# A two-layer decoder trunk on one core: from a planned order to the order of the program

## The chip, the core and the metric

The kernel runs on one core of a Trainium2 chip. The core has five engines that work side by side, each through its own list of instructions, in the order of that list: TensorE (PE) multiplies matrices and writes to PSUM; VectorE (DVE), ScalarE (ACT) and GpSimd (POOL) work element by element; SyncE (SP) issues the DMA transfers. POOL cannot read PSUM. Semaphores tie the lists together where one instruction needs the result, or the freed buffer, of another. The metric is the device time of one execution in microseconds (us).

## What is computed

Two layers work on x, 2048 tokens of 1024 channels, in float32. Cut to what matters:

```python
def _even_layer(x, ...):                       # layer 0
    q, k, v, g_a, a_lr, u, sv, g_b = _split(x @ w_in, EVEN_SIZES)
    log_a = log_sigmoid(a_lr @ w_a2 + b_a) / 16.0          # forget gate
    o = _gla(q, k, v, log_a)                   # gated linear attention
    o_a = _head_rmsnorm(o, g) * silu(g_a)
    o_b = _spatial_gating(gelu(u), gelu(sv), ...) * silu(g_b)
    return _layer_norm(ALPHA * x + concatenate([o_a, o_b]) @ w_out, ...)

def _odd_layer(x, positions, ...):             # layer 1
    q, k, v, g_c, p, g_d = _split(x @ w_in, ODD_SIZES)
    o = _retention(_rotary(q), _rotary(k), v)  # S <- gamma^128 S + k^T v per chunk
    o_c = _head_groupnorm(o, g) * silu(g_c)
    o_d = _multiscale_pool(p, w_pool, scale) * silu(g_d)
    return _layer_norm(ALPHA * x + concatenate([o_c, o_d]) @ w_out, ...)
```

The weights are 1024 x 3088 and 1024 x 3072 for the way in, and 1024 x 1024 twice for the way out. GLA's state and the retention's state are carried from each chunk of tokens to the next.

## The kernel before

**Blocks, units, passes.** The tokens are worked in four blocks of 512; each block goes through layer 0 and then layer 1. A layer is a row of products of [512 x 1024] by [1024 x 512], called units, run by `unit` (L159). A unit has four chunks of 128 (tokens or output channels), each a sum over eight slices of the contraction, `kt`. To keep float32's accuracy on the faster format, each operand is held as a rounded part and a rest, and each product is three matmuls (`PASSES`, L147): so a unit is 4 x 8 x 3 = 96 matmuls of 512 columns. With `width=2` two chunks share a sweep over the slices; with `width=1` (the second half of each output projection, and layer 1's q, k) each chunk has a sweep of its own. The order of the units in a block: v with the low-rank gate (272 columns), the other half of v (256 columns), q and k of GLA, sv, u and g_b, g_a ("the GLA gate unit"), the rest of g_b and u, the two halves of the output projection with LayerNorm; then layer 1: q and k, v, pooling with its gate, the retention's gate, pooling again, output projection with LayerNorm.

**Weight slices.** One slice, [128 x 512] of a weight, serves 12 matmuls. `wslice` (L93) fetches it into one of 7 raw buffers and `split` (L85) turns it into the two parts: ACT rounds (L87), DVE or POOL by turns subtracts (L91). The parts lie in `wpool`, 12 tiles. `next_weights` (L120) asks for slices up to 20 ahead; a tile comes free when the last matmul on its slice is through, which is in the last sweep of a unit.

**Pauses.** Small steps are put between the matmuls by `later(fn, delay)` (L129) and `between` (L132), which `product` and `unit` call every 24 matmuls. Such steps are: `turn`, the transposes of a row tile after LayerNorm (L556 to L564, 8 transposes on PE, then ACT and DVE make the two parts) and of layer 1's q and k (L589); the low-rank gate (L407) and the decay (L362: Abs, Exp, Ln on ACT; then per half of the heads a subtraction, a scan and an end on DVE, and three exponentials on ACT, L377 to L389); the attention steps `first` and `outputs` (L329, L334); `sgu` (L504); the gates (L183).

**LayerNorm.** `layer_norm_out` (L189) evacuates each chunk of the output projection on DVE: scale and add (L199), statistics (L200, L203), two steps over 1024 columns (L208, L210). Between the two POOL computes the reciprocal root (L178, L181).

**Attention state.** Each step of four updates the state `s0` or `s1`. In GLA `upd` (L455) decays, adds, and decays again; a third copy of the queries, scaled by the decay at mid-chunk, is made on POOL (L435) and used against the state. In layer 1 the queries carry powers of gamma and the keys the inverse powers (L579).

**What sets the order.** Every engine's list is made at build time by a planner: it takes the program's order as priority, estimates how long each instruction takes, and puts each where it can run by that estimate. So the weight splits, asked for at the start of a unit, are placed wherever the planner sees a free tile and a free engine. The constants, and the cosine and sine tables of the rotary step (L283 to L306, some 20 DVE instructions), stand at the start of the program.

Of the kernel before, what the change touches and what calls it, by code (L numbers as in the profile page):

```python
# [9 lines left out]
F32 = mybir.dt.float32  # L10
# [18 lines left out]
PAD = 480  # L29

# [20 lines left out]
def trunk(ctx, tc, x, xT, pos, wv, w, w_a2, pvec, rowp, sgu_rows, w_sT, w_pool, ropec, poolc, out):  # L51
# [6 lines left out]
    wpool = ctx.enter_context(tc.tile_pool(name="wpool", bufs=12))  # L58
# [9 lines left out]
    ps_s = ctx.enter_context(tc.tile_pool(name="ps_s", bufs=2, space=PSUM))  # L68

# [23 lines left out]
    def wslice(*src):  # L93

        raw = rawp.tile([P, 512], F32, tag="raw", name="raw")
        t = wpool.tile([P, 2, 512], F32R, tag="w", name="wt")
        width, c = src[0].shape[1], 0
        for s in src:
            nc.sync.dma_start(raw[:, c:c + width], s)
            c += width  # L100
        split(raw[:, 0:c], t[:, 0, 0:c], t[:, 1, 0:c])
        return [t[:, :, i * width:(i + 1) * width] for i in range(len(src))]

    def xslice(b, kt, units):
        raw = rawp.tile([P, 512], F32, tag="raw", name="xraw")
        nc.sync.dma_start(raw, xT[b, kt])
        split(raw, units[kt // 4][:, kt % 4, 0, :], units[kt // 4][:, kt % 4, 1, :])

    def act_unit():
        return acts.tile([P, 4, 2, TB], F32R, tag="T", name="T")  # L110
# [6 lines left out]
    ready = []  # L117
# [31 lines left out]
    def product(ps, chunks):  # L149

        for kt in range(KT):
            for p_, (lhs, rhs) in zip(ps, chunks):
                for n, (a, b) in enumerate(PASSES):
                    nc.tensor.matmul(p_, lhsT=lhs(kt, a), rhs=rhs(kt, b),  # L154
                                     start=(kt == 0 and n == 0), stop=(kt == KT - 1 and n == 2))
            if len(ps) > 1 and (kt + 1) % (KT // len(ps)) == 0 and kt < KT - 1:
                between()

    def unit(xs, wt, evac, token_major, width=2, cols=512):  # L159

        def chunk(n):
            sl = slice(n * P, (n + 1) * P)
            if token_major:
                return (lambda kt, a: xs[kt // 4][:, kt % 4, a, sl]), (lambda kt, b: wt[kt][:, b, :])
            return (lambda kt, a: wt[kt][:, a, sl]), (lambda kt, b: xs[kt // 4][:, kt % 4, b, :])

        for n in range(0, 4, width):
            ps = [big() for _ in range(width)]
            product([p_[:, 0:cols] for p_ in ps], [chunk(n + i) for i in range(width)])
            for i, p_ in enumerate(ps):  # L170
                evac(n + i, p_[:, 0:cols])
            between()

    def rstd(dst, var, eps, scale=1.0):

        n = dst.shape[1]
        if scale == 1.0:
# [3 lines left out]
        nc.gpsimd.tensor_tensor(dst, dst, neghalf[:, :n], op=ALU.pow)  # L181

    def gate(dst_u, h, psT, gain, sil):  # L183
# [33 lines left out]
    xunits = [act_unit(), act_unit()]  # L217
    for kt in range(KT):
        xslice(0, kt, xunits)
        ready.extend(wslice(*stream.pop(0)))  # L220
# [25 lines left out]
    nc.sync.dma_start(pv, pvec)  # L246
# [3 lines left out]
    wa2raw = w2("wa2raw")[0:48, 0:256]  # L250
# [521 lines left out]
```

## Time and profile before

| | |
|---|---|
| median of 3 runs | 1538.36 us (1537.05 to 1538.57) |
| the profiled execution | 1536.12 us, its span 1533.7 us |
| PE busy | 1490.2 us, 97% |
| DVE, ACT, POOL busy | 832.4, 568.1, 637.3 us (54%, 37%, 42%) |
| DMA | 162.19 MB, mean 106 GB/s |
| matmuls of L154 | 3456 and 2688, 731.0 and 625.7 us busy |
| weight rounding on ACT (L87, into wt) | 496 instructions, mean 616 ns |
| weight subtraction on POOL, on DVE (L91, into wt) | 252 of mean 1381 ns, 244 of mean 896 ns |

The profile is that of one execution. Its span runs from the first to the last instruction. A busy PE is not PE at its peak, since matmuls are pipelined and their ends are modelled; what PE waits for is read from the idle time ahead of its instructions. A group's row gives the line in the kernel, engine, operation, what it writes and reads, the count, then busy time in us and mean ns of one, then idle time of the engine ahead of it and what ended it. In a timeline a row gives start, length in us, engine, line, operation.

### The profile page before, as it was taken

To read this page: it belongs to the slowest core of one execution; us is meant where nothing else is said; L and a number is where in the kernel's file an instruction comes from. 1 tells how busy PE (TensorE), PEld (TensorE's weight loads), DVE (VectorE), ACT (ScalarE), POOL (GpSimd) and SP (SyncE) were. 2 spreads that over 40 slices of the span, in tenths; PEclk is the share of its full clock that TensorE was granted. 3 is DMA by queue.
4 is the path that set the end of the run, shared out by engine and by line. 5 is a ranking of instruction groups with operands and counts; after the bars stand their busy time and mean duration, and the time that the engine had idled before them with its cause. 6 is when DMAs were issued, how large, how long until landed. Compare 5 with 4: busy or idle time off the path is not lost.

```text
span 1533.7 us, 21008 instructions
## 1 busy us (share of the span) xinstructions
PE 1490.2 (97%) x7728; PEld 1245.4 (81%) x7728; DVE 832.4 (54%) x1491; ACT 568.1 (37%) x949; POOL 637.3 (42%) x568
## 2 busy tenths in 40 slices
PE   7999999999999999999999999999999999989997
PEld 6888877888888887788888888778888888877886
DVE  6554384645745348464574525746466542573635
ACT  4634322333443332324263332323436334232430
POOL 5245433445524443335443443434543444242542
PEclk9999999999999999999999999999999999999999
DMA  7325322234523431323352242131444334223231
GB/s 227 101 83 165 91 75 83 69 104 133 179 69 98 150 111 55 98 68 115 121 179 83 83 160 87 55 110 56 128 136 150 107 100 144 62 69 97 79 94 55
DMA packets 87047, 162.19 MB, mean 106 GB/s; under 512 B 10096, under 2 KB 18336, under 8 KB 86944
## 3 DMA queue, kind: packets, MB, share of 16 engines
q1 hardware_dynamic: 86944, 160.85, 33.9%
q8 instruction: 60, 0.98, 0.3%
q14 instruction: 43, 0.35, 0.1%
HBM read 152.43 MB, written 8.39 MB: 105 GB/s over the span
## 4 chain that ended last, share of the span: by engine, by line
PE 87%; DVE 6%; issue 4%; POOL 2%; ACT 1%; DMA 0%; SPq 0%; POOLq 0%; DVEq 0%; ACTq 0%
PE big L154 77%; PE att L312 4%; DVE wt L91 2%; PE trp L348 1%; PE trp L508 1%; PE trp L560 1%; PE trp L643 1%; DVE ra L584 1%; DVE rows L210 1%; DVE ra L586 0%; DVE ang L299 0%; PE trp L535 0%; PE trp L679 0%; DVE ra L579 0%; DVE alr L403 0%
## 5 line engine op out<-in xcount | busy, mean ns | idle before, releaser
L154 PE MATMUL big<-wt,T 128*128 128x512 f32 (+2 forms) x3456 | 731.0, 371 | 6.2 <-ACT wt L87 4.5
L154 PEld LDWEIGHTS big<-wt,T 128*128 128x128 f32 x3456 | 601.1, 190 | 114.2 <-ACT wt L87 4.5
L154 PE MATMUL big<-T,wt 128*128 128x512 f32 x2688 | 625.7, 391 | 0.0
L154 PEld LDWEIGHTS big<-T,wt 128*128 128x128 f32 x2688 | 500.6, 188 | 106.3 <-issue 2.7
L91 POOL TENSOR_TENSOR wt<-raw,wt 128x512 fp32r<-128x512 f32 (+1 forms) x252 | 345.7, 1381 | 350.5 <-ACT wt L87 350.2
L87 ACT ACTIVATE wt<-raw 128x512 fp32r<-128x512 f32 (+1 forms) x496 | 301.9, 616 | 322.8 <-PE big L154 288.3
L91 DVE TENSOR_TENSOR wt<-raw,wt 128x512 fp32r<-128x512 f32 (+1 forms) x244 | 217.1, 896 | 249.7 <-ACT wt L87 248.6
L91 POOL TENSOR_TENSOR T<-y,T 128x512 fp32r<-128x512 f32 x48 | 61.0, 1289 | 75.9 <-ACT T L87 75.9
L199 DVE SCALAR_TENSOR_TENSOR rows<-rows,big 128x512 f32<-128x512 f32 x64 | 43.6, 683 | 79.9 <-PE big L154 79.9
L178 POOL TENSOR_SCALAR lnrs<-lnmv 128x1 f32<-128x1 f32 x32 | 26.6, 832 | 119.2 <-DVE lnmv L203 119.1
L327 DVE COPY_PREDICATED pm<-mask,att 128x256 f32<-128x256 int32 x64 | 26.0, 440 | 65.4 <-PE att L312 65.4
L562 ACT ACTIVATE T<-trp 128x512 fp32r<-128x512 f32 x32 | 17.5, 596 | 102.0 <-PE trp L560 102.0
L210 DVE SCALAR_TENSOR_TENSOR rows<-rows,lnrs,ln 128x1024 f32<-128x1024 f32 (+1 forms) x36 | 47.1, 1318 | 13.5 <-POOL lnrs L181 11.9
L186 DVE SCALAR_TENSOR_TENSOR y<-trp,pv,sg 128x512 f32<-128x512 f32 x48 | 34.8, 745 | 34.6 <-PE trp L679 17.6
L181 POOL TENSOR_TENSOR rs<-rs,neghalf 128x4 f32<-128x4 f32 x48 | 49.3, 1028 | 4.0
L178 POOL TENSOR_SCALAR rs<-mv 128x4 f32<-128x4 f32 x32 | 7.4, 231 | 100.8 <-DVE mv L488 52.6
L208 DVE SCALAR_TENSOR_TENSOR rows<-rows,lnmv,ln 128x1024 f32<-128x1024 f32 (+1 forms) x36 | 45.2, 1266 | 0.7
L91 POOL TENSOR_TENSOR T<-pd,T 128x512 fp32r<-128x512 f32 x16 | 25.7, 1606 | 42.5 <-ACT T L87 42.5
L200 DVE BATCH_NORM_STATS2 lnst<-rows 128x6 f32<-128x512 f32 x64 | 42.9, 687 | 0.9
L87 ACT ACTIVATE T<-y 128x512 fp32r<-128x512 f32 x48 | 30.4, 632 | 31.2 <-DVE y L186 30.9
L651 ACT ACTIVATE pb<-big 128x512 f32<-128x512 f32 x16 | 9.6, 599 | 85.4 <-PE big L154 78.7
L520 ACT ACTIVATE act<-big 128x512 f32<-128x512 f32 x32 | 19.1, 597 | 52.3 <-PE big L154 51.5
(185 smaller groups left out, 1085.0 us busy)
## 6 DMA issues: line engine op xcount, KB each, us to landing
raw<-in_w SPq DMA_DIRECT2D x448, 256.0 KB, 2.8
xraw<-in_xT SPq DMA_DIRECT2D x32, 256.0 KB, 3.1
rows<-in_x SPq DMA_DIRECT2D x8, 1024.0 KB, 6.0
ln<-in_rowp SPq DMA_DIRECT2D x16, 512.0 KB, 5.6
out<-rows SPq DMA_DIRECT2D x12, 512.0 KB, 2.6
raw<-in_wv SPq DMA_DIRECT2D x32, 136.0 KB, 3.2
raw<-in_wv SPq DMA_DIRECT2D x32, 128.0 KB, 2.6
out<-rows SPq DMA_DIRECT2D x8, 256.0 KB, 2.0
```

The costliest lines, as they stand in the source:

```text
L87: nc.scalar.activation(hi, src, AF.Copy)
L91: eng.tensor_tensor(lo, src, hi.bitcast(F32), op=ALU.subtract)
L154: nc.tensor.matmul(p_, lhsT=lhs(kt, a), rhs=rhs(kt, b), start=(kt == 0 and n == 0), stop=(kt == KT - 1 and n == 2))
L178: nc.gpsimd.tensor_scalar(dst, var, eps, None, op0=ALU.add)
L181: nc.gpsimd.tensor_tensor(dst, dst, neghalf[:, :n], op=ALU.pow)
L186: nc.vector.scalar_tensor_tensor(y, psT, gain, sil, op0=ALU.mult, op1=ALU.mult)
L199: nc.vector.scalar_tensor_tensor(rh, rh, ALPHA, ps, op0=ALU.mult, op1=ALU.add)
L200: nc.vector.bn_stats(sts[t][:, half, :], rh)
L208: nc.vector.scalar_tensor_tensor(row[:, cs], row[:, cs], mv[:, 0:1], gt[:, cs], op0=ALU.subtract, op1=ALU.mult)
L210: nc.vector.scalar_tensor_tensor(row[:, cs], row[:, cs], rs, bt[:, cs], op0=ALU.mult, op1=ALU.add)
L312: nc.tensor.matmul(dst, lhsT=lhsT, rhs=rhs, start=start, stop=stop, skip_group_check=True)
L327: nc.vector.copy_predicated(pm[t % 2][:, r::2, :], mask_b, ps[r][:, 2:4, :])
```

## The change

Each engine now issues in the order in which the program emits its instructions (`tc.manual_schedule()`), and the program is rewritten for that order.

- **Weights.** `fetch` issues one slice's DMA, `cut` splits the oldest one landed and fetches another. `pace`, called after each slice's matmuls, adds a twelfth of a credit per matmul of 512 columns (less for narrower ones), up to 3, and cuts a slice per credit while one of the 12 tiles has room. A unit that finds no slice ready cuts one on the spot. In the second half of each output projection, all subtractions go to POOL (`sub=nc.gpsimd`).
- **Pauses.** The turns after LayerNorm and of layer 1's q, k have delay 3, not 2. The splits of the gates and the SGU are put off by one pause. The decay is in two steps, `decay` up to Ln and `decay2`, which has the subtractions and scans of both halves first and then the exponentials.
- **State.** GLA's state is kept decayed to the middle of the next chunk, so the third copy of the queries and POOL's product go; `upd` is one addition and one multiplication by a joined factor `f`. In layer 1 the queries no longer carry powers of gamma; the group norm takes them out, and its epsilon is scaled instead (`ret_eps`). The q half of the evacuation is a copy on ACT, the k half a multiplication on DVE. In `outputs`, the scaling of the result comes after the mask for the next step.
- **Start.** The first block's x and weight slices are issued first, then the small constants with five weight slices among them; the constants' arithmetic comes in pauses of the second v unit, and the cosine and sine in pauses after GLA's q, k, three instructions at a time.
- **Next x.** The next block's x is fetched two slices ahead and split in four steps of two.

The diff, cut to its core:

```diff
+SLOTS = 12
+    ctx.enter_context(tc.manual_schedule())
...
-    AHEAD = KT + 12
-    def next_weights():
-        while len(ready) < AHEAD and stream:
-            ready.extend(wslice(*stream.pop(0)))
-        return [ready.pop(0) for _ in range(KT)]
...
+    landed, ready = [], []
+    room, credit = [SLOTS], [0.0]
+    cutter = [None]
...
+    def cut():
+        raw, n, width = landed.pop(0)
+        assert room[0] > 0
+        room[0] -= 1
+        t = wpool.tile([P, 2, 512], F32R, tag="w", name="wt")
+        c = n * width
+        split(raw[:, 0:c], t[:, 0, 0:c], t[:, 1, 0:c], cutter[0])
+        ready.extend((t[:, :, i * width:(i + 1) * width], i == n - 1) for i in range(n))
+        fetch()
+    def pace(matmuls):
+        credit[0] = min(credit[0] + matmuls / 12.0, 3.0)
+        while credit[0] >= 1.0 and room[0] > 0 and landed:
+            cut()
+            credit[0] -= 1.0
...
+    def unit(xs, evac, token_major, width=2, cols=512, sub=None):
+        cutter[0] = sub
+        wt = []
+        for n in range(0, 4, width):
+            ps = [big()[:, 0:cols] for _ in range(width)]
+            for kt in range(KT):
+                if len(wt) == kt:
+                    while not ready:
+                        cut()
+                    wt.append(ready.pop(0))
...
+                if n + width == 4 and last:
+                    room[0] += 1
+                pace(3 * width * cols / 512.0)
+                if width > 1 and (kt + 1) % (KT // width) == 0 and kt < KT - 1:
+                    between()
             for i, p_ in enumerate(ps):
-                evac(n + i, p_[:, 0:cols])
+                evac(n + i, p_)
             between()
...
     def gate(dst_u, h, psT, gain, sil):
...
-        split(y, dst_u[:, h, 0, :], dst_u[:, h, 1, :], nc.gpsimd)
+        later(lambda: split(y, dst_u[:, h, 0, :], dst_u[:, h, 1, :], nc.gpsimd))
...
-        unit(xs, next_weights(), lambda t, ps: evac(0, t, ps), True)
-        unit(xs, next_weights(), lambda t, ps: evac(1, t, ps), True, width=1)
+        unit(xs, lambda t, ps: evac(0, t, ps), True)
+        unit(xs, lambda t, ps: evac(1, t, ps), True, width=1, sub=nc.gpsimd)
@@ outputs(t)
-            norm(t, [p_[:, 0:2, :] for p_ in ps])
-            upd(t, u[:, 0:2, :])
+            scale = norm(t, [p_[:, 0:2, :] for p_ in ps])
+            nc.vector.tensor_tensor(state, state, u[:, 0:2, :], op=ALU.add)
+            upd(t)
             if not last:
                 masked(t + 1, ps)
+            scale()
@@ gla_exps (the second part of gla_decay)
+            out.append((tb, ta, e2, ends))
+        for tb, ta, _, ends in out:
             nc.scalar.activation(tb, ta, AF.Exp, scale=1.0 / 16.0)
             nc.scalar.activation(ta, ta, AF.Exp, scale=-1.0 / 16.0)
             nc.scalar.activation(ends, ends, AF.Exp, scale=1.0 / 16.0)
@@ layer0
+        if b == 0:
+            constants()
+            later(constants2, 3)
+            later(constants3, 4)
         later(low_rank, 1)
         later(decay, 2)
-        unit(xs, next_weights(), lambda t, ps: nc.scalar.activation(vt[:, t, 256:512], ps, AF.Copy), True, cols=256)
+        later(decay2, 3)
+        unit(xs, lambda t, ps: nc.scalar.activation(vt[:, t, 256:512], ps, AF.Copy), True, cols=256)
...
-            nc.gpsimd.tensor_tensor(G[:, 3, :].rearrange("p (t c) -> p t c", c=P),
-                                    G[:, 0, :].rearrange("p (t c) -> p t c", c=P),
-                                    ends[:, :, 0:1].broadcast_to([P, NT, P]), op=ALU.mult)
...
-        def upd(t, u):
-            for s in range(2):
-                ends = decays[s][2]
-                nc.vector.scalar_tensor_tensor(s0[:, s, :], s0[:, s, :], ends[:, t, 0:1], u[:, s, :],
-                                               op0=ALU.mult, op1=ALU.add)
-                nc.vector.tensor_scalar(s0[:, s, :], s0[:, s, :], ends[:, t, 1:2], None, op0=ALU.mult)
+        def upd(t):
+            nc.vector.tensor_tensor(s0, s0, f[:, :, t:t + 1].broadcast_to([P, 2, P]), op=ALU.mult)
@@ after, and evac_qk of layer1
-            later(turn, 2)
+            later(turn, 3)
@@ evac_qk of layer1
-            nc.vector.tensor_tensor(a.rearrange("p (h c) -> p h c", c=64), ps.rearrange("p (h c) -> p h c", c=64),
-                                    gam.unsqueeze(2).broadcast_to([P, 8, 64]), op=ALU.mult)
+            nc.scalar.activation(a[:, 0:256], ps[:, 0:256], AF.Copy)
+            nc.vector.tensor_tensor(a[:, 256:512].rearrange("p (h c) -> p h c", c=64),
+                                    ps[:, 256:512].rearrange("p (h c) -> p h c", c=64),
+                                    gam[:, 4:8].unsqueeze(2).broadcast_to([P, 4, 64]), op=ALU.mult)
```

More of the change, by code (lines that the diff above doesn't have):

```diff
@@ L91, in split @@
         eng.tensor_tensor(lo, src, hi.bitcast(F32), op=ALU.subtract)
[L93 to L110, printed above, removed]
     stream = []
@@ L147, in trunk @@
     PASSES = ((0, 0), (0, 1), (1, 0))
[L149 to L165, printed above, removed]
-        for n in range(0, 4, width):
-            ps = [big() for _ in range(width)]
-            product([p_[:, 0:cols] for p_ in ps], [chunk(n + i) for i in range(width)])
+    def unit(xs, evac, token_major, width=2, cols=512, sub=None):
+        cutter[0] = sub
+        wt = []
+        for n in range(0, 4, width):
+            ps = [big()[:, 0:cols] for _ in range(width)]
[4 more added lines that the diff above has]
+                    wt.append(ready.pop(0))
+                t, last = wt[kt]
+                for i, p_ in enumerate(ps):
+                    sl = slice((n + i) * P, (n + i + 1) * P)
+                    xt = xs[kt // 4][:, kt % 4]
+                    for q, (a, b) in enumerate(PASSES):
+                        lhsT, rhs = (xt[:, a, sl], t[:, b, :]) if token_major else (t[:, a, sl], xt[:, b, :])
+                        nc.tensor.matmul(p_, lhsT=lhsT, rhs=rhs, start=(kt == 0 and q == 0),
+                                         stop=(kt == KT - 1 and q == 2))
+                if n + width == 4 and last:
[3 more added lines that the diff above has]
+                    between()
             for i, p_ in enumerate(ps):
-                evac(n + i, p_[:, 0:cols])
+                evac(n + i, p_)
             between()
@@ L272, in trunk @@
     cst = const.tile([P, 4, P], F32, name="cst")
-    sb = w2("sgub")
-    nc.sync.dma_start(sb, sgu_rows[0:1, :].broadcast_to([P, TB]))
-    sbs = w2("sgubs")
-    nc.sync.dma_start(sbs, sgu_rows[1:2, :].broadcast_to([P, TB]))
-    ps = tr()
-    for g in range(4):
-        nc.tensor.matmul(ps[:, g, :], lhsT=sb[:, g * P:(g + 1) * P], rhs=wsT[:, g, :], start=True, stop=True)
-    nc.vector.tensor_tensor(flat(cst), flat(ps), sbs, op=ALU.add)
     cos = const.tile([P, SEQ // P, 32], F32, name="cos")
@@ new lines, in trunk @@
+    wraw, sb, sbs = w2("wraw"), w2("sgub"), w2("sgubs")
+    xunits = [act_unit(), act_unit()]
+    for kt in range(KT):
+        raw = xfetch(0, kt)
+        fetch()
+        xcut(raw, kt, xunits)
+        raw, _, width = landed.pop(0)
+        t = wpool.tile([P, 2, 512], F32R, tag="w", name="wt")
+        split(raw[:, 0:width], t[:, 0, 0:width], t[:, 1, 0:width])
+        room[0] -= 1
+        ready.append((t[:, :, 0:width], True))
+    nc.sync.dma_start(pv, pvec)
+    for i in range(3):
+        nc.sync.dma_start(wa2raw[16 * i:16 * i + 16, :], w_a2)
@@ new lines, in constants2, with constants3 @@
+    def constants2():
+        split(wraw, wp[:, 0, :], wp[:, 1, :], nc.vector)
+        for g in range(4):
+            nc.gpsimd.affine_select(out=wsT[:, g, :], in_=wsT[:, g, :], compare_op=ALU.is_ge, fill=0.0,
+                                    base=0, pattern=[[1, P]], channel_multiplier=-1)
+        nc.vector.scalar_tensor_tensor(ret_eps, gam[:, 4:8], 64.0 * LN_EPS, gam[:, 4:8], op0=ALU.mult, op1=ALU.mult)
+    def constants3():
+        ps = tr()
+        for g in range(4):
+            nc.tensor.matmul(ps[:, g, :], lhsT=sb[:, g * P:(g + 1) * P], rhs=wsT[:, g, :], start=True, stop=True)
+        nc.vector.tensor_tensor(flat(cst), flat(ps), sbs, op=ALU.add)
@@ L341, in outputs @@
                     b0 = 64 * r
-                    mm(ps[r][:, s, :], qk(s, b0, t)[2], state[b0:b0 + 64, s, :], stop=last and s == 1)
+                    mm(ps[r][:, s, :], qk(s, b0, t)[1], state[b0:b0 + 64, s, :], stop=last and s == 1)
             if not last:
@@ L396, in layer0 @@
         alrT = w2("alrT")[0:48, :].bitcast(F32R)
-        als, decays, heads = [], [], {}
+        als, logs, decays, heads = [], [], [], {}
+        f = small.tile([P, 2, NT], F32, tag="f", name="f", bufs=2)
         def evac_v0(t, ps):
```

186 lines of the change are left out of this document (112 added, 74 removed).

## The prediction

> **What bounds the kernel now.** I read the page first, then the waits of TensorE (PE), then the timeline at the places where PE waits and where the new order puts something else in front of it.
>
> ```profile
> span 1533.7 us, 21008 instructions
> ...
> PE 87%; DVE 6%; issue 4%; POOL 2%; ACT 1%; DMA 0%; SPq 0%; POOLq 0%; DVEq 0%; ACTq 0%
> ```
>
> The profiled execution took 1536.1 us, 2.4 above its span and 2.2 below the median of the runs (1538.4). The chain that ended last is PE for 87%. No matmul is added or removed, so only PE's waits can change the time.
>
> ```profile
> PE trp L560 <- issue: 11.4, 4, 2.9
> PE trp L410 <- DVE alr L403: 6.8, 7, 1.3
> PE trp L592 <- DVE ra L586: 5.5, 6, 1.0
> PE big L154 <- ACT wt L87: 4.5, 1, 4.5
> PE trp L592 <- ACT wt L87: 2.0, 2, 1.0
> PE trp L560 <- DVE rows L210: 1.6, 2, 0.8
> PE trp L279 <- POOL wsT L266: 1.6, 1, 1.6
> ```
>
> These are PE's waits: total us, times, longest. The 4.5 is the start, which stays. The other six rows make 28.9 us: the transposes after layer 0's LayerNorm (L560), those of layer 1's queries and keys (L592), the low-rank gate (L410), the SGU constant (L279).
>
> ```profile
> 209.25 5.92 PE L154 MATMUL big<-wt,T 128*128 128x512 f32 x25
> 218.03 1.06 PE L560 MATMUL trp<-ident,rows 128*128 128x128 f32 x8 [2.86 <-issue]
> 218.85 7.33 PE L154 MATMUL big<-wt,T 128*128 128x512 f32 x24
> ```
>
> Columns: start, length, work. After the wait of 2.86, 24 matmuls take 7.33 where 25 took 5.92: 1.6 us of slower clock, which happens behind two of these four waits, 3 us. And the last matmul before a wait is drawn longer than its turn takes, which hides some 0.2 to 0.3 of each of about 25 waits, an estimate of 6. If every wait after the start went, the kernel would lose about 38 us.
>
> **The change part by part.**
>
> *What goes.* The turns (transposes) come a chunk of 24 matmuls, 5.5 us, later; the cosine and sine chain leaves the start; the bursts of weight splitting after a unit end. I count all 38 as removed and add back what I find late in the new order. In the first block PE still waits for its PSUM tiles after the first product, since four evacuations now follow the weight slices on ACT: +2 (0 to 3).
>
> *What paces the weights now.* I followed the credit through the text: a slice is split per 12 matmuls of 512 columns, per 22 or so of the narrower v units. After the two v units only two slices of the next unit (layer 0's q and k) have been issued in blocks 1 and 2, the second of them behind the exponentials; three in block 3 and four in block 0, the last of each behind them too.
>
> ```profile
> 403.04 3.74 ACT L87 ACTIVATE wt<-raw 128x512 fp32r<-128x512 f32 x7
> ...
> 413.39 0.74 ACT L419 ACTIVATE v<-big 128x256 f32<-128x256 f32 x2 [1.92 <-PE big L154]
> 414.17 0.69 ACT L368 ACTIVATE ta<-trp,pv 128x512 f32<-128x512 f32 x1
> 414.87 1.28 ACT L372 ACT_TABLE_LOAD   x1
> 416.17 0.63 ACT L372 ACTIVATE ta<-ta 128x512 f32<-128x512 f32 x1
> ```
>
> ```profile
> 414.30 6.02 PE L154 MATMUL big<-wt,T 128*128 128x256 f32 x48
> 420.16 16.52 PE L154 MATMUL big<-T,wt 128*128 128x512 f32 x72
> ```
>
> ```profile
> 425.86 0.69 DVE L377 TENSOR_TENSOR tb<-tb,ta 128x512 f32<-128x512 f32 x1 [1.00 <-ACT ta L374]
> 426.58 1.22 DVE L378 TENSOR_TENSOR_SCAN ta<-smask,tb 128x512 f32<-128x512 bf16 x1
> 427.84 0.17 DVE L382 COPY ends<-ta 128x8 f32<-128x8 f32 x1
> 428.05 0.43 DVE L384 TENSOR_TENSOR ta<-ta,ends 128x256 f32<-128x256 f32 x1
> ```
>
> Before, seven slices were split in one go at 403, long ahead (first row). Now count from 413.39, the evacuation between the halves of the second v unit. ACT issues, in order: two copies 0.74, two Abs 1.4, a table load 1.28, two Exp 1.26, a load 1.28, two Ln 1.26 (the Exp row's 0.63 each). That is 7.2. Only then comes the rounding of the q unit's first slice, 0.5 to 0.6 (3.74 for seven): 7.8; its subtraction stands on POOL in blocks 1 and 2 and takes 1.38 (the group row below): 9.2. PE is done with the second v unit at 420.16, which is 6.8, and uses the subtracted half two matmuls (0.23 each, 16.52 for 72) later, at 7.2. **First wait: 2.0.**
>
> The second slice stands behind the decay exponentials. DVE can start at the first Ln, 6.6, and needs 2.6 for each of two heads' pairs (four rows above, start to end): 9.2 and 11.8. ACT's last two Exp and a short one end at 13.3, the slice's rounding at 13.9, its subtraction on DVE (0.7) at 14.6. PE, released at 9.2 and busy 0.9, wants that half at 10.5. **Second wait: 4.1**, and 1 to 2 more where POOL's subtraction and DVE's scan get in each other's way (below). I take 6.5 per block for 1 and 2. In block 3 the first two slices are in time and the third has the same place, with its subtraction on POOL: 6.7. In block 0 it is the fourth slice, with constants to split besides: 5. Together **+25 (20 to 29)**. Evacuations queued behind the exponentials free PSUM tiles that PE needs only a pass later. Four waits of 4 us and over would bring the slow clock of 1.6 in most cases: +4 (0 to 10).
>
> ```profile
> 196.85 0.69 DVE L199 SCALAR_TENSOR_TENSOR rows<-rows,big 128x512 f32<-128x512 f32 x1 [2.84 <-PE big L154]
> 197.57 0.69 DVE L200 BATCH_NORM_STATS2 lnst<-rows 128x6 f32<-128x512 f32 x1
> 198.30 0.21 DVE L203 BATCH_NORM_AGGREGATE lnmv<-lnst 128x2 f32<-128x12 f32 x1
> 198.54 1.28 DVE L208 SCALAR_TENSOR_TENSOR rows<-rows,lnmv,ln 128x1024 f32<-128x1024 f32 x1
> 200.62 1.28 DVE L210 SCALAR_TENSOR_TENSOR rows<-rows,lnrs,ln 128x1024 f32<-128x1024 f32 x1 [0.79 <-POOL lnrs L181]
> ```
>
> ```profile
> 213.82 5.24 POOL L91 TENSOR_TENSOR wt<-raw,wt 128x512 fp32r<-128x512 f32 x3
> ```
>
> ```profile
> 215.65 2.28 DVE L210 SCALAR_TENSOR_TENSOR rows<-rows,lnrs,ln 128x1024 f32<-128x1024 f32 x1
> ```
>
> *LayerNorm and layer 1's q, k.* A row tile's LayerNorm takes DVE 5.05 us (196.85 to 201.90) of a pass of 5.5. While POOL subtracts without pause (1.75 each instead of 1.3 to 1.4), the last step takes 2.28 instead of 1.28. The new order puts eight subtractions of the LayerNorm's second unit on POOL, two per pass, right behind the reciprocal root that releases this step. So I count 6.05 a pass: 0.6 of lag per pass, and with the turn's two PSUM subtractions the third turn finds its PSUM tiles taken for about 1 us. Then one slice of layer 1's q, k unit is subtracted on DVE behind all that: 1 to 2.5. **+11 over four blocks** (5 to 22), against 20.5 in the L560 and L592 rows.
>
> *The v unit of the next block.* Its seventh slice is issued behind the last row tile's root on POOL, its eighth behind the last step on DVE; the root ends some 5 us after the pass (0.1 to 3.9 in these rows, plus lag), the subtraction 1.4 later, and PE wants it at 4.5 to 4.8 (36 matmuls of 6.02/48): 1 to 2.7 in three blocks, **+4** (2 to 8).
>
> ```profile
> L91 POOL TENSOR_TENSOR wt<-raw,wt 128x512 fp32r<-128x512 f32 x232 | 329.4, 1430 | 337.2 <-ACT wt L87 336.9
> ...
> L181 POOL TENSOR_TENSOR rs<-rs,neghalf 128x4 f32<-128x4 f32 x48 | 49.3, 1028 | 4.0
> ...
> L469 DVE TENSOR_REDUCE ss<-sq 128x4 f32<-128x512 f32 x16 | 10.9, 684 | 23.3 <-ACT sq L467 23.3
> ...
> L467 ACT ACTIVATE sq<-att 128x256 f32<-128x256 f32 x32 | 10.5, 381 | 38.9 <-PE att L312 38.9
> ```
>
> ```profile
> 125.60 1.54 PE att L312 x16
> ```
>
> *The GLA gate unit.* (Group rows: busy, mean ns; the mean of all slice forms is 1.38.) At its first pause stand the last attention step, then two deferred SGU splits, then the pending weight slices. From the pause: attention 1.54, two squares 0.76, the sum 0.68, the root 1.03 with a short scaling ahead, all waiting for one another: 4.2 on POOL; two SGU subtractions and the seventh slice's, 1.3 to 1.4 each: 8.2. PE wants it 12 matmuls after the attention's 2.1, plus 0.45: 5.3. A wait of 2.9 in blocks 1 and 2, 1.5 in block 0, none in block 3: **+7** (5 to 9). Two smaller places of the same kind (the output projection's fifth slice behind the last SGU split, the gate unit before it): +3 (0 to 3).
>
> *At nothing.* The state's new form saves POOL's product and a DVE pass per step, and moves half of an evacuation to ACT; these lie beside matmuls. If that cover failed, each costs under 1 us per step. Layer 1's other units start with six slices issued, so nothing queued matters there. The cosine and sine steps go three per pause beside the sv unit and the next ones, where DVE has time and nothing waits for them before layer 1. On SP five slices stay in hand; the constants' loads now queue behind the first slices, and stores of the output ahead of later ones for less than a pass.
>
> Sum: -38 + 2 + 25 + 4 + 11 + 4 + 7 + 3 = +18 on the profiled 1536.1, so 1554, and 1556 beside the median.
>
> **A rule that would price it otherwise.** The rows of POOL at 5.24 for three and DVE at 2.28 show both still moving while they overlap, each slowed. The Trainium skill (SBUF — State Buffer, "Who interferes with whom") says that a VectorE instruction with two SBUF inputs and a GpSimd instruction that reads SBUF take the shared port pair in turn, and that the second one is blocked until the first is through. By that rule the last step would wait for a whole subtraction.
>
> **Rivals.**
>
> - *Slower, moderate (the forecast)*: slices reach PE late behind ACT's exponentials. For it: the order of ACT's queue and the durations. Against: nothing in the trace of before shows the order itself.
> - *Faster*: the waits of 38 go, and the order costs less than I count because POOL, DVE and ACT seldom collide (ACT is busy 37%): 20 at the q unit, 5 at the LayerNorm, 2 in the start and v units, 3 at the gate, no slow clock: 1538 - 38 + 30 = 1530. If the slices of the q unit were in time after all, it would be 1510. Deciding point: whether a slice's rounding must wait for the Ln of its block.
> - *Much slower*: POOL and DVE exclude each other in the LayerNorm units. Per pass two steps of 1.28, a root of 0.8 and two subtractions of 1.3 are 6.0 against 5.45, and each blocked step adds 1.3: about 0.6 per pass more than counted, 32 passes, 18 us: 1574. It decides once DVE's row tile exceeds 6.1 us. The skill's rule above would lead here.
> - *It doesn't do what it says*: the written order nearly equals the planner's, or the parts cancel: 1538.
>
> **How the numbers follow.** Forecast 0.49, much slower 0.20, faster 0.25, no change 0.06. About 0.2% (3 us) is what a measurement of this kernel can tell. So slower 0.69, same 0.06, faster 0.25. The forecast alone runs from 1540 to 1572; the range takes in most of the faster case and of the slower: 1518 to 1584.
>
> **What would show it.** Right: PE's waits name ACT's or DVE's weight slices at the start of layer 0's q, k unit, 5 to 8 us per block, with ACT's exponentials just before; L560, L592 and L410 nearly gone. Wrong: no wait of PE over 1 us there, and PE's share above 98%. The LayerNorm step is right if L210 takes 1.8 to 2.3 us in the second unit; the gate step if PE waits for a POOL subtraction some 12 us after it begins.

## The result, and the profile after

The kernel after takes 1588.9 us (median of 4 runs, 1586.3 to 1590.6) where the kernel before takes 1538.2 beside it: a ratio of 1.0329, interval 1.0312 to 1.0347. It is slower, as forecast, but by 51 us where 18 were forecast, and it lies above the range. The profiled execution took 1590.6 us. From its page, the span, the busy time of the engines and the chain that ended last:

```profile
span 1588.9 us, 20834 instructions
...
PE 1515.9 (95%) x7728; PEld 1259.0 (79%) x7728; DVE 841.1 (53%) x1452; ACT 529.6 (33%) x956; POOL 702.0 (44%) x592
...
PE 70%; DVE 9%; POOL 8%; issue 6%; DMA 3%; ACT 2%; SPq 1%; POOLq 0%; ACTq 0%; DVEq 0%
```

PE does the same 7728 matmuls, but is busy 25.7 us longer than before (1490.2), and idle for 73.0 us of its span where it was for 43.5. The waits of PE, total, times, longest:

```profile
PE big L186 <- ACT wt L91: 23.5, 9, 5.6
PE big L186 <- POOL wt L95: 20.7, 17, 3.3
PE big L186 <- DVE wt L95: 10.6, 10, 2.1
PE trp L631 <- DVE T L634: 5.9, 4, 1.5
PE big L186 <- ACT v L464: 3.5, 1, 3.5
```

The waits of before at L560, L592 and L410 are gone, but for the 5.9 at L631, the turn. In their place stands one kind: a weight slice that is not yet rounded (L91) or subtracted (L95). Where the time went, by the kind of unit: from the start of a unit's first matmul to that of the next unit's (for the last one, to the end of the span), summed over the four blocks, in us. The last column is an experiment told below (e14); units that moved by less than 0.5 are left out.

| unit | before | after | e14 |
|---|---|---|---|
| both v units, layer 0 | 116.5 | 114.5 | 112.4 |
| q, k, layer 0 | 89.6 | 118.9 | 91.4 |
| u and g_b, first half | 116.2 | 117.6 | 116.2 |
| GLA gate unit | 103.6 | 117.6 | 103.6 |
| output projection, first half | 87.4 | 99.7 | 87.4 |
| output projection, second half, with LayerNorm | 94.3 | 101.3 | 97.2 |
| q, k, layer 1 | 121.9 | 112.4 | 103.9 |
| v, layer 1 | 108.3 | 105.9 | 106.0 |
| layer 1's output projection, second half | 95.1 | 99.9 | 95.5 |

*Layer 0's q, k unit in block 1.* From the timeline: start, length, engine, line, work, and in brackets the idle time just before with what ended it.

```profile
424.75 1.28 ACT L425 ACT_TABLE_LOAD   x1
427.21 1.28 ACT L427 ACT_TABLE_LOAD   x1
428.50 1.15 ACT L427 ACTIVATE ta<-ta 128x512 f32<-128x512 f32 x2
429.56 0.61 ACT L91 ACTIVATE wt<-raw 128x512 fp32r<-128x512 f32 x1
430.23 0.73 PE L186 MATMUL big<-T,wt 128*128 128x512 f32 x2 [0.64 <-ACT wt L91]
430.25 1.93 POOL L95 TENSOR_TENSOR wt<-raw,wt 128x512 fp32r<-128x512 f32 x1 [11.28 <-ACT wt L91]
432.23 1.20 PE L186 MATMUL big<-T,wt 128*128 128x512 f32 x4 [1.27 <-POOL wt L95]
435.89 0.63 ACT L446 ACTIVATE ta<-ta 128x512 f32<-128x512 f32 x1
436.52 0.61 ACT L91 ACTIVATE wt<-raw 128x512 fp32r<-128x512 f32 x1
437.19 10.17 PE L186 MATMUL big<-T,wt 128*128 128x512 f32 x34 [3.76 <-ACT wt L91]
```

The rounding at 429.56 stands behind two table loads and the Ln at 428.50; PE waits 0.64 for it and 1.27 for its subtraction. The next rounding, at 436.52, stands behind the last exponentials (L446 at 435.89), and PE waits 3.76. POOL had been idle for 11.28: it had no subtraction to do, because ACT had not come to the rounding.

*The clock.* Stretches of that unit: length, PE busy and its matmuls, the granted clock, DMA share, GB/s.

```profile
437.00:444.00 7.00, 6.81 (x20) 0.65 0.51 159
444.00:451.00 7.00, 7.00 (x32) 1.00 0.42 140
```

PE is busy in both, and does 20 matmuls in the first and 32 in the second. Over the whole span, after and then before:

```profile
core 0: 1588.9 us, clock 0.981
```

```profile
core 0: 1533.7 us, clock 0.996
```

An estimate from these two means: a clock lower by 0.019 over 1588.9 is 30.2 us, by 0.004 over 1533.7 it is 6.1. The difference, 24, is nearly all of the 25.7 us by which PE is busy longer.

*The gate unit in block 1.*

```profile
523.28 0.66 ACT L533 ACTIVATE sq<-att 128x256 f32<-128x256 f32 x2 [7.13 <-PE att L363]
523.97 0.69 DVE L535 TENSOR_REDUCE ss<-sq 128x4 f32<-128x512 f32 x1 [4.10 <-ACT sq L533]
524.74 0.19 POOL L205 TENSOR_SCALAR rs<-ss 128x4 f32<-128x4 f32 x1 [6.03 <-DVE ss L535]
525.02 1.29 POOL L206 TENSOR_TENSOR rs<-rs,neghalf 128x4 f32<-128x4 f32 x1
526.28 2.95 POOL L95 TENSOR_TENSOR T<-ys,T 128x512 fp32r<-128x512 f32 x2
529.20 1.26 POOL L95 TENSOR_TENSOR wt<-raw,wt 128x512 fp32r<-128x512 f32 x1
530.51 4.15 PE L186 MATMUL big<-T,wt 128*128 128x512 f32 x10 [3.27 <-POOL wt L95]
```

POOL idles until 524.74 for the sum, then does the root, two SGU subtractions, and last the slice that PE waits for. The ten matmuls after the wait of 3.27 take 4.15, at about half rate.

*The first half of the output projection.*

```profile
568.51 1.28 ACT L591 ACT_TABLE_LOAD   x1 [7.51 <-PE big L186]
573.59 0.63 ACT L91 ACTIVATE T<-ys 128x512 fp32r<-128x512 f32 x1 [2.70 <-DVE ys L584]
576.17 0.63 ACT L91 ACTIVATE T<-ys 128x512 fp32r<-128x512 f32 x1 [1.95 <-DVE ys L584]
576.71 3.74 ACT L91 ACTIVATE wt<-raw 128x512 fp32r<-128x512 f32 x7
577.37 0.49 PE L186 MATMUL big<-wt,T 128*128 128x512 f32 x1 [1.03 <-ACT wt L91]
579.89 10.49 PE L186 MATMUL big<-wt,T 128*128 128x512 f32 x45 [2.02 <-POOL wt L95]
```

ACT waits 2.70 and 1.95 for the products of the last two SGU parts, whose splits stand ahead of seven weight slices in its list; then it does all seven in one go.

*The second half, with the LayerNorm.*

```profile
601.75 0.69 DVE L224 SCALAR_TENSOR_TENSOR rows<-rows,big 128x512 f32<-128x512 f32 x1 [3.38 <-PE big L186]
605.45 1.29 POOL L95 TENSOR_TENSOR wt<-raw,wt 128x512 fp32r<-128x512 f32 x1
605.52 2.31 DVE L235 SCALAR_TENSOR_TENSOR rows<-rows,lnrs,ln 128x1024 f32<-128x1024 f32 x1 [0.79 <-POOL lnrs L206]
606.71 2.28 POOL L95 TENSOR_TENSOR wt<-raw,wt 128x512 fp32r<-128x512 f32 x1
...
613.23 5.73 PE L186 MATMUL big<-wt,T 128*128 128x512 f32 x24
620.42 1.25 PE L631 MATMUL trp<-ident,rows 128*128 128x128 f32 x8 [1.46 <-DVE T L634]
628.77 0.73 PE L186 MATMUL big<-wt,T 128*128 128x512 f32 x2 [1.92 <-DVE wt L95]
630.67 6.81 PE L186 MATMUL big<-wt,T 128*128 128x512 f32 x24
```

DVE's row tile takes 6.08 us (601.75 to 607.83), its last step (L235) 2.31 beside POOL's two subtractions. The third turn waits 1.46, and one slice is late by 1.92.

### The profile page after: what moved, and what is told of

The parts are those of the page before. It is cut to its first block, busy times and chain, and to the rows that moved or that the text cites. A ratio compares the mean times of both kernels' runs of the same rounds, so it can differ in the third digit from the quotient of the medians.

```text
span 1588.9 us, 20834 instructions
## 1 busy us (share of the span) xinstructions
PE 1515.9 (95%) x7728; PEld 1259.0 (79%) x7728; DVE 841.1 (53%) x1452; ACT 529.6 (33%) x956; POOL 702.0 (44%) x592
## 4 chain that ended last, share of the span: by engine, by line
PE 70%; DVE 9%; POOL 8%; issue 6%; DMA 3%; ACT 2%; SPq 1%; POOLq 0%; ACTq 0%; DVEq 0%
PE big L186 61%; PE att L363 4%; DVE rows L235 3%; DMA xraw<-in_xT 3%; POOL wt L95 2%; POOL lnrs L203 2%; POOL T L95 2%; DVE lnst L225 1%; DVE rows L224 1%; POOL lnrs L206 1%; PE trp L399 1%; DVE wt L95 1%; DVE T L634 1%; PE trp L631 1%; DVE ys L584 1%
## 5 line engine op out<-in xcount | busy, mean ns | idle before, releaser
L186 PE MATMUL big<-T,wt 128*128 128x512 f32 x2688 | 642.4, 397 | 29.2 <-ACT wt L91 17.0
L186 PEld LDWEIGHTS big<-T,wt 128*128 128x128 f32 x2688 | 508.5, 191 | 144.0 <-ACT wt L91 19.1
L95 POOL TENSOR_TENSOR wt<-raw,wt 128x512 fp32r<-128x512 f32 (+1 forms) x284 | 401.4, 1424 | 369.8 <-ACT wt L91 363.1
L95 DVE TENSOR_TENSOR wt<-raw,wt 128x512 fp32r<-128x512 f32 x212 | 228.8, 1086 | 181.5 <-ACT wt L91 181.3
L91 ACT ACTIVATE wt<-raw 128x512 fp32r<-128x512 f32 (+1 forms) x496 | 279.5, 610 | 115.3 <-PE big L186 69.7
L224 DVE SCALAR_TENSOR_TENSOR rows<-rows,big 128x512 f32<-128x512 f32 x64 | 43.5, 679 | 89.7 <-PE big L186 89.7
L203 POOL TENSOR_SCALAR lnrs<-lnmv 128x1 f32<-128x1 f32 x32 | 39.9, 1248 | 91.0 <-DVE lnmv L228 91.0
L95 POOL TENSOR_TENSOR T<-y,T 128x512 fp32r<-128x512 f32 x48 | 73.7, 1556 | 8.4 <-ACT T L91 8.4
L235 DVE SCALAR_TENSOR_TENSOR rows<-rows,lnrs,ln 128x1024 f32<-128x1024 f32 (+1 forms) x36 | 64.3, 1785 | 24.9 <-POOL lnrs L206 24.7
L95 POOL TENSOR_TENSOR T<-pd,T 128x512 fp32r<-128x512 f32 x16 | 20.7, 1292 | 64.1 <-ACT T L91 64.1
L533 ACT ACTIVATE sq<-att 128x256 f32<-128x256 f32 x32 | 10.5, 381 | 98.2 <-PE att L363 98.2
L689 DVE BATCH_NORM_STATS2 st<-att 128x6 f32<-128x128 f32 x64 | 14.2, 284 | 54.5 <-PE att L363 54.5
L580 POOL TENSOR_TENSOR act<-act 128x512 f32<-128x512 f32 x16 | 20.4, 1296 | 38.4 <-ACT act L591 38.4
```

The source lines that it names most:

```text
L91: nc.scalar.activation(hi, src, AF.Copy)
L95: eng.tensor_tensor(lo, src, hi.bitcast(F32), op=ALU.subtract)
L186: nc.tensor.matmul(p_, lhsT=lhsT, rhs=rhs, start=(kt == 0 and q == 0), stop=(kt == KT - 1 and q == 2))
L224: nc.vector.scalar_tensor_tensor(rh, rh, ALPHA, ps, op0=ALU.mult, op1=ALU.add)
L235: nc.vector.scalar_tensor_tensor(row[:, cs], row[:, cs], rs, bt[:, cs], op0=ALU.mult, op1=ALU.add)
L580: nc.gpsimd.tensor_tensor(gu, gu, sg, op=ALU.mult)
```

## The experiments

Three theories. **A**: the slices are emitted too late, so that they stand behind other work in the lists of ACT, POOL and DVE. **B**: work that went to POOL collides with DVE. **C**: the rate alone starves PE, whatever ACT has to do. All ratios are to the kernel before, run beside it on the same chip. Of a kernel without a ratio there is a single run, so a few us of it show nothing.

**e1: a whole credit per column tile, however narrow.**

```diff
-                pace(3 * width * cols / 512.0)
+                pace(3 * width)
```

> Theory A (slices are issued too late, behind other work in ACT's and POOL's queues): counting every matmul of the two narrow v units as a full one puts 12 slices instead of 2 to 4 ahead of GLA's q, k, and 10 instead of 4 or 5 ahead of each later unit of layer 0. The q, k units fall from 118.9 us (four blocks) to about 90, the GLA gate units from 117.6 to about 104, the first halves of layer 0's output projection from 99.7 to about 88; in all about 1588.9 - 52 = 1537. Theory B (the work moved to POOL and its collisions with DVE cost the time): the number of subtractions is the same, so the waits stay and the time is above 1575.

1524.3 us, ratio 0.9912 (0.9895 to 0.9929): one expression takes away 65 us, more than the 52 expected. The q, k unit is at 90.1, the gate unit at 103.6, the first half of the projection at 87.4. These three make 55 of the 65. B, the collision of POOL's subtractions with the LayerNorm's row tile, cannot give that: the LayerNorm's second unit itself got only 4.3 shorter, and L235 still takes 2.3 in half of layer 0's row tiles. Block 0's first v unit gets 9 us longer, because its evacuations on ACT now stand behind slices that have not landed.

**e3: the gate's and the SGU's splits at once, not a pause later.**

```diff
-        later(lambda: split(y, dst_u[:, h, 0, :], dst_u[:, h, 1, :], nc.gpsimd))
+        split(y, dst_u[:, h, 0, :], dst_u[:, h, 1, :], nc.gpsimd)
...
-            later(lambda: split(y, cb[:, g, 0, :], cb[:, g, 1, :], nc.gpsimd))
+            split(y, cb[:, g, 0, :], cb[:, g, 1, :], nc.gpsimd)
```

> Splits of the gates and the SGU are issued at once, not a pause later. Theory A: in the GLA gate unit two POOL subtractions (2.95 us) leave the place between the attention step's root and the seventh weight slice, so these units fall from 117.6 to 105 to 108 us and the whole to about 1578; the q, k units stay at 119. Theory B: the same POOL work, so within 3 us of 1589.

1578.1 us. The gate unit goes from 117.6 to 106.6, so the two deferred splits were most of what stood ahead of its slice; the q, k unit stays at 119.1, and the first half of the projection gets longer (102.6).

**e4: the planner back, with the rewritten text.** The line `ctx.enter_context(tc.manual_schedule())` is left out.

> The new text, but ordered by the planner (the one line that asks for the order of the program is left out). Theory A: the planner moves rounding and subtraction of slices ahead of the waiting exponentials; the q, k units come back to about 90, and with the later turns the whole is 1515 to 1540. Theory B (the text's pacing, state and POOL moves are at fault, not the order): above 1570.

1520.3 us, ratio 0.9886 (0.9872 to 0.9901). The text is no loss under the planner; the text taken as the order is.

**e5: no Exp and Ln in the decay, and so no table loads there.** The three Exp and the Ln of the decay become Abs.

> The decay's Exp and Ln are replaced by Abs, which needs no table load; the decay comes out as a constant, so the output is not the reference's. Theory A: ACT's chain ahead of the first late slice is two loads (2.56 us) shorter and that ahead of the second about as much; the first wait of the q, k unit goes and the second falls from 3.9 to about 1.5, so these units fall from 118.9 to 100 to 107, with fewer slow-clock stretches; the whole is about 1573. Theory C (the credit alone starves PE there, whatever ACT does): no change of the q, k units.

1578.0 us; the q, k unit takes 109.1, more than the 100 to 107 expected, and so gets back about a third of the 29.3 that it had lost; the gate unit is unchanged at 117.5. How long ACT's chain is counts, so C falls as a whole; but the shorter chain does not bring the slices in time.

**e6: the subtractions beside the LayerNorm by turns on DVE and POOL again.**

```diff
-        unit(xs, lambda t, ps: evac(1, t, ps), True, width=1, sub=nc.gpsimd)
+        unit(xs, lambda t, ps: evac(1, t, ps), True, width=1)
```

> The kernel after the change, with one thing undone: in the units beside the LayerNorms and in layer 1's q,k unit the slices' subtractions alternate between VectorE and POOL again. If the subtractions on POOL slow the LayerNorm's row tile on VectorE (theory B), the LayerNorm's second unit of layer 0 (101.3 us after, 94.3 before) comes back to 94 to 96 and layer 1's to 95 to 97, the time to 1575 to 1580. If it is the late issue (theory A), the second unit stays within 2 us of 101.3, since VectorE then has the row tiles and half of the subtractions to do, or gets longer, and the time is 1586 to 1600.

1600.1 us; the LayerNorm's second unit 105.9, longer than with the change (101.3). Sharing the subtractions out again is no cure. But the edit does not take the collision away: one subtraction on POOL still stands beside L235, which takes 2.28 to 2.31 in all sixteen row tiles of layer 0, as with the change. What speaks against B as the cause is e1, and e14 below, where L235 takes 2.3 in twelve of the sixteen and the 51 us are gone all the same.

**e7: e1's rate, but low in the first v unit of block 0.**

```diff
-                pace(3 * width * cols / 512.0)
+                pace(3 * width * (cols / 1024.0 if width == 4 else 1.0))
```

> The kernel after the change with two edits of the rate: a slice per matmul counted whole (three credits of a twelfth for each column tile, whatever its width), but in the first v unit of each block only by its columns over 1024. With a whole credit throughout, 1524.3 us were measured, of which block 0's first v unit lost 9 us to evacuations behind slices whose transfers had not landed. If that wait came from the credit alone, it goes: that unit is 18 to 21 us in block 0 where 27.5 were seen, and the time is 1512 to 1518. If the evacuations wait on the transfers however the slices are issued, it stays at 1522 to 1526.

1518.0 us, ratio 0.9874 (0.9858 to 0.9891); block 0's first v unit 15.7, where e1 had 27.5. Only that unit has `width == 4`, so the rate is low in block 0 alone and not, as the expectation words it, in the first v unit of each block.

**e8: e7 and e6 together.**

> As the run with the rate edited at both places, and the subtractions beside the LayerNorms alternate again. With the slices ahead, theory B's part should show alone: the second LayerNorm unit of layer 0 was 97.0 us with the whole credit and 94.3 before, its turns waiting 5.8 us in sum on VectorE's copies. B: 94 to 95 and the turns' wait under 3, the time 3 to 5 us below the run beside it. If the collision is worth nothing there: within 1 us of it, or above.

1518.2 us, ratio 0.9875 (0.9860 to 0.9890): the same as e7, with 98.6 in the LayerNorm's unit beside 98.1. Once the slices are in time, which engine subtracts there is worth nothing that can be measured. What the collision itself costs is not shown: L235 takes 2.3 in 13 of the 16 row tiles in e7 and still in 11 in e8.

**e9: e7 with the turns two chunks behind again.** `later(turn, 3)` becomes `later(turn, 2)` at both places.

> As the run with the rate edited at both places, but the turns of the LayerNorm's row tiles and of layer 1's q and k stand two chunks behind their unit's evacuation as in the kernel before, not three. Layer 1's q,k unit was 121.9 us before, 112.4 after the change and 103.8 with the whole credit. If the later turn is what shortened it, it is back at 115 to 122 us here, and the second LayerNorm unit gets longer by several us too: time 1528 to 1545. If the slices did it, it stays at 104 to 108 and the time within 5 us of the run beside it.

1519.7 us: layer 1's q, k unit stays at 105.7, and the LayerNorm's unit takes 102.0 where e7 takes 98.1. In the written order with slices on hand the later turn is worth a few us at most (1.7 by these runs).

**e10 and e11: a stock given once.** `unit` gets an argument `extra`, added to what `pace` is given; only block 0's second v unit passes one, 3.0 a step (four slices more by its end) or 1.5 (two).

> The kernel after the change, its rate untouched (a slice per twelve matmuls of full width, exactly what the units use up), but in block 0's second v unit, once in the whole program, four slices more are issued. Theory A in its sharper form says that the place in the queues is set by how many slices are on hand, and that a rate equal to the use keeps whatever stock there is, so that one gift of four lasts for all four blocks: layer 0's q,k unit 90 to 93 us in each sum, gate unit 104 to 106, the first LayerNorm unit 87 to 90, time 1516 to 1526. If the whole credit helped because it speeds up the issue anew in each block, this gift is used up in block 0, blocks 1 to 3 keep their waits, and the time is 1575 to 1582.

> The same with a gift of two slices in block 0's second v unit, and nothing else. Two slices are some 5 us of matmuls at the first pass over a unit's weights, against waits of 0.8, 1.4 and 3.9 us in the q,k unit and of 3.3 us in the gate unit: by the sharper theory A the gate and LayerNorm waits go (gate unit 104 to 107 us, first LayerNorm unit 88 to 92) and the q,k unit keeps a part (93 to 105), time 1525 to 1550, and the half-rate stretches that follow the waits go with them (PE busy 1490 to 1500 us, where it was 1515.9). If the stock does not matter: 1583 to 1590.

e10: 1582.4 us, ratio 1.0295 (1.0280 to 1.0311); e11: 1594.6, above both of its ranges. The theory in this form falls, and shows how. In block 0 the gift does all that was hoped (e10: q, k 24.5 where after has 28.6, gate 25.9 for 29.8, projection 21.9 for 25.7). In blocks 1 to 3 little is left of it (e10: q, k 29.2, 31.8, 29.7). A count through the text shows a leak. All units are credited with as many slices as they use, but one: the first v unit uses eight and is credited 8 x 272 / 512 = 4.25. So 3.75 are lost per block. In the kernel after they come back through `while not ready: cut()`, by the same count four times in each of blocks 1 to 3, two in layer 0's q, k unit and two in its LayerNorm's: each cut at the moment of need, behind all that the engines have in hand.

**e12: the later turns alone, in the kernel before.** `later(turn, 2)` becomes `later(turn, 3)` at L564 and L595, nothing else.

> The kernel before the change, with one part of the change alone: the turns of the LayerNorm's row tiles and of layer 1's q and k are put a chunk later (a delay of three where it was two). The prediction held that this takes away the waits of PE at these transposes, 20.6 us in the groups of before. If so, layer 1's q,k unit goes from 121.9 us to 104 to 110 and the time to 1518 to 1526. If the shorter unit comes from the order as written or from the evacuation of q and k shared with ScalarE, the unit stays above 115 and the time within 5 us of 1537.

1517.3 us, ratio 0.9871 (0.9854 to 0.9887). The waits of PE at the transposes:

```profile
PE trp L410 <- DVE alr L403: 7.4, 6, 1.8
...
PE trp L560 <- DVE T L563: 3.3, 4, 0.8
```

L592 is gone, L560 at 3.3 from 13.0; layer 1's q, k unit takes 103.1. This one number at two places brings as much as the best written order below (e14), to within the intervals. It need not be the same gain: in the written order, e9 puts the number back and loses next to nothing.

**e13: the planner with e7's rate.**

> The rewritten text with the compiler's planner ordering the engines (the line that fixes the order left out), and the rate whole but low in the first v unit. The planner alone gave 1520.3 us, the rate alone 1518.0. If the planner moves the slices wherever the text puts them, the rate changes little: 1517 to 1521. If their gains add (the planner's LayerNorm unit of 93.9 us against 98.1, layer 1's q,k 104.8 against 106.6, and no late start in block 0), 1510 to 1515.

1513.95 us, ratio 0.9848 (0.9834 to 0.9863), below e4's interval; it overlaps e12's. The lowest median here; layer 1's q, k unit is at 100.9.

**e14, e15, e16: the leak closed**, with a gift of four, of two, and none (`extra` 3.0, 1.5, absent).

```diff
-                pace(3 * width * cols / 512.0 + extra)
+                pace(3 * width * (1.0 if cols == 272 and width == 2 else cols / 512.0) + extra)
```

> The kernel after the change with the gift of four slices in block 0's second v unit, and the first v unit of blocks 1 to 3 credited for the slices that it uses up (8, where the text gives 4.25 for its 272 columns). Counted through the text, eight slices are then on hand at the start of nearly every unit of all blocks. If the stock was drained at that place alone, blocks 1 to 3 now do what block 0 did with the gift (q,k unit 24.5, gate unit 25.9, first LayerNorm unit 21.9 us): q,k 89 to 94 in sum, gate 103 to 105, LayerNorm 87 to 89, time 1514 to 1522. If it is something else in blocks 1 to 3: 1560 to 1580.

> The same with a gift of two: six slices on hand at the start of nearly every unit. In block 0, where the gift of two was still on hand, the q,k unit took 23.5 us, the gate unit 25.9 and the first LayerNorm unit 21.9. If a stock of six is enough, all blocks are like that: q,k 92 to 97 in sum, gate 103 to 105, time 1520 to 1532. If only eight is: 1535 to 1575.

> Only the rate of the first v unit of blocks 1 to 3 repaired, no gift. By count block 0 has four or five slices on hand as after the change, blocks 1 to 3 have six. So block 0 should keep its q,k unit of 28.6 us, gate unit of 29.8 and LayerNorm unit of 25.7, and blocks 1 to 3 go to 23 to 24.5, 25.9 and 21.9: time 1588.9 less about 20, 10 and 8, and a few us of the last units: 1540 to 1553. If the rate there does not matter without a gift: above 1575.

e14: 1515.8 us, ratio 0.9851 (0.9835 to 0.9868). With the leak closed the same gift of four lasts: blocks 1 to 3 have a q, k unit of 22.3 each. Its page and PE's waits:

```profile
PE 1489.3 (98%) x7728; PEld 1247.1 (82%) x7728; DVE 820.9 (54%) x1456; ACT 539.9 (36%) x956; POOL 686.6 (45%) x588
```

```profile
PE trp L632 <- DVE T L635: 6.0, 8, 1.1
PE big L186 <- ACT wt L91: 4.4, 1, 4.4
PE big L186 <- ACT v L464: 3.8, 1, 3.8
PE trp L326 <- POOL wsT L317: 2.5, 3, 1.8
PE big L186 <- POOL wt L95: 0.4, 1, 0.4
```

The slices are out of the list but for the start and 0.4 us, and PE is busy 26.6 us less than after.

e15: 1552.8 us, in the span named for a stock that is not enough. Six on hand do for the gate unit (103.6) and the projection's first half (87.4), but less well for layer 0's q, k unit (98.9, more than the 92 to 97 expected), and not for the units of one chunk at a time, which use eight slices within their first 24 matmuls: the LayerNorm's unit is at 101.3, layer 1's at 104.1, its q, k at 112.0. e16: 1552.9 us, ratio 1.0093 (1.0074 to 1.0111); block 0 keeps its 28.6, 29.8 and 25.7 to the digit, blocks 1 to 3 take 24.0, 25.9 and 22.8. Of the 51 us that the change lost, closing the leak alone takes 36 away, and a stock of eight the rest and more. Seven was not tried.

## Why the prediction was right or wrong

Right in sign and in the main mechanism, slices late behind other work in the lists; wrong in size. e14 differs from after only in the credit, and so in the slices on hand; its span of 1514.6 splits what was measured: e14 less before is what the rest of the change brings, after less e14 is what late slices cost. PE's idle time is its span less its busy time (after 73.0, e14 25.3). The forecast missed the sum by 37.2 us: 18.9 by what goes and 22.6 by the slow clock, less 4.3. "Only PE's waits can change the time", the prediction began; nearly half of the 55.2 is matmuls that ran slower, their number unchanged.

| | forecast | measured |
|---|---|---|
| what goes | -38 | -19.1 (1514.6 - 1533.7) |
| new waits | +52 | +47.7 (73.0 - 25.3) |
| slow clock | +4 | +26.6 (1515.9 - 1489.3) |
| sum | +18 | +55.2 |

- *What goes, -38: too much.* L560, L592 and L410 went as forecast, but e14 shows 6.0 at the turn, 3.8 at the first evacuations and 2.5 at the SGU constant in their place. The idle time fell by 18.2 (43.5 to 25.3), not by 28.9. And the 6 us said to be hidden in matmuls drawn too long before a wait, with 3 of clock, do not show in the sum: PE is busy 1490.2 before and 1489.3 in e14. In layer 1's q, k unit its busy time did fall by 5.1, but it rose elsewhere, by 1.9 in layer 0's q, k unit and 1.2 in the LayerNorm's; why is open. The most that any run took off the span is 21.5 (e13, 1512.2).
- *Layer 0's q, k unit, +25 and 4 of clock: met in sum, by luck.* First wait forecast at 2.0 in blocks 1 and 2: 0.64 and 1.27 in block 1. Second at 4.1 and up: 3.76. The unit lost 29.3, but 18.5 of it is idle time and 10.8 slower matmuls: the waits were counted too long and the clock too short. The deciding point of the faster rival, whether the rounding must wait for the Ln, is at 428.50 and 429.56: it does.
- *Slow clock, +4: the step that failed most.* It was put behind four waits of 4 us. It came in every block behind shorter ones too, such as the 3.27 of the gate unit, and 1.92 at 628.77. The rows shown ahead of the forecast had such a case, 2.86 with 1.6 us lost, on two of four; it was carried to one unit instead of to all new waits. Put at +4, it measured +26.6.
- *The gate unit, +7: the waits held, the clock was missed.* The order on POOL was as worked out, 3.27 for 2.9 in block 1, but some 2 us of slow matmuls came on top (5.2 and 4.9 in all in blocks 1 and 2), and block 0 lost 3.9 where 1.5 was forecast: +14.1, of which 8.5 is idle time.
- *Two smaller places, +3: a quarter.* They cost 1.4 and 12.2. Missed was ACT's wait for the products of the last SGU parts (2.70 and 1.95), with seven slices in its list behind them. Only the last split on POOL was counted.
- *LayerNorm and layer 1's q, k: +11 on one side and the L560 and L592 rows on the other.* Counted were 20.5 and 3 of clock away and 11 back, -12.5; the two units gave +7.0 and -9.5. The row tile is 6.08 where 6.05 was worked out, the turn waits 1.46, the slice 1.92: these were right. In e14, with slices on hand, the two units give -15.1. So late slices cost 12.6 in them, 4.1 in the LayerNorm's unit and 8.5 in layer 1's q, k, where the forecast had one slice of 1 to 2.5 us a block.
- *Next block's v unit, +4; start, +2.* Layer 1's second LayerNorm unit and the v units together gave +2.8, with the wait of 3.5 for evacuations at the start, where the two terms less L410 and L279 made -2.4. "Layer 1's other units start with six slices issued, so nothing queued matters there" failed for its second LayerNorm unit: +4.8 with six or seven on hand, +0.4 in e14 with eight.
- *The much slower rival*, POOL and DVE shutting each other out: the mechanism is there, the price is not. POOL's subtraction at 605.45 takes 1.29, as if alone; the step L235, started 0.07 later, ends 1.08 after it; and POOL's next one, 2.28 long, ends 1.15 after the step. They take turns. By the rule of the Trainium skill (SBUF — State Buffer, "Who interferes with whom") the second instruction is blocked until the first is through; this trace agrees. The prediction read "both still moving" from a mean: its 5.24 for three subtractions is 1.35, 1.70 and 2.25, each of the later two ending 1.1 after DVE's instruction before it. But the 2.28 that the forecast took for the step holds that wait already, and the first step met no subtraction (1.29 at most), so the row tile stays at 6.08, under the rival's 6.1. In e14 one row tile of layer 0 in each block takes 6.7, at 1515.8 us, so the length of the row tile does not decide. The rival came near the time for another reason.

What stays open: why a turn two chunks behind is in time in e9 and not in the kernel before. The order of the lists differs, and so does the evacuation of q and k, half of it on ACT; no run separates the two. Nor is it shown which of e13's parts, beyond the later turn, are worth the 3 us to e12, which the intervals don't tell apart.

## What to carry to other kernels

Where the program's order is the order of issue, a producer paced by its consumer's use keeps its stock and never builds one, so count made against used for every unit: one narrow unit that used eight and was credited 4.25 cost 36 of 51 us. The stock must cover the longest piece of foreign work in the producer's list and the fastest use: here eight slices were enough for units that use eight in 24 matmuls, and six were not. And try the parts of a large change alone: one delay, from two to three, gave 1517.3 us, nearly all that the best version gave.

## What the runs showed of the hardware

- Waits of PE well below 3 us brought half the clock. After 1.92 us at 628.77 and the transposes that follow, 24 matmuls took 6.81 where 24 at 613.23 took 5.73. In a row for each microsecond, the granted clock stands behind the count of matmuls:

```profile
631.00:632.00 1.00, 1.00 (x4) 0.50 0.00 0
632.00:633.00 1.00, 1.00 (x4) 0.51 0.03 8
633.00:634.00 1.00, 1.00 (x6) 1.00 0.00 0
```

The Trainium skill (TensorE: Matmul & The Clock Gate, "HAM oscillation — how this bites in real kernels") warns of idle gaps over about 3.4 us; here shorter ones did it, and the measurement decides. Equal waits were not followed alike: the 2.86 of before slowed the clock in two blocks of four, and behind the 2.02 at 579.89 no slow stretch follows (45 matmuls in 10.49).
- POOL's subtraction and DVE's step with two inputs in SBUF took turns, as told above of the much slower rival: 2.31 us instead of 1.28 for the step, 2.28 instead of 1.29 for the second subtraction.
- A table load can itself stand behind a result. Two groups of loads on ACT, after and then before: count, busy us, mean ns, idle time of ACT ahead of them.

```profile
L591 ACT ACT_TABLE_LOAD x8 | 10.3, 1283 | 30.1 <-PE big L186 30.0
```

```profile
L520 ACT ACT_TABLE_LOAD x8 | 10.3, 1283 | 0.1
```

In the planned order the loads ran straight behind other work; in the written order ACT idled 30.1 us in sum until PE's result was there and loaded then. In e14, with that idle time still 16.8, the unit behind it is as short as before (87.4), so this idle time alone did not lengthen the unit.
